# Grouped-query attention: all turns of an odd unit ahead of its second scores

## The chip, the core and the metric

The kernel runs on one core of a Trainium2 chip. The metric is the device time of one execution in microseconds (us). Five instruction streams work side by side and meet at semaphores: TensorE (PE in the rows; PEld is its weight loads), VectorE (DVE), ScalarE (ACT), GpSimd (POOL) and SyncE (SP), which issues most DMAs. TensorE writes its results to PSUM, eight banks of 128 x 512 float32 values here, from where VectorE or ScalarE has to read them before the bank can be written anew.

## The reference, cut to what matters

A two-layer diffusion trunk: layer 0 has neighbourhood attention, layer 1 grouped-query attention (GQA), each followed by a gated ConvFFN. The change touches only the GQA of the 512 latent tokens in layer 1, 16 query heads of width 64 over 4 key heads, with 512 latent and 128 context keys in one softmax:

```
q, k, v = gqa_qkv(h, w_qkv, q_norm, k_norm)      # 512 tokens
q, k = axial_rope(q), axial_rope(k)
k_all = concat([k, cache_k]); v_all = concat([v, cache_v])   # 640 keys
s = einsum('bqkgd,bskd->bkgqs', q, k_all) * hd ** -0.5
p = softmax(s, axis=-1)
o = einsum('bkgqs,bskd->bqkgd', p, v_all)
```

## The kernel before, in words

The latent GQA is cut into 32 units (`NU = 2 * H`). A unit is one head and 256 of the 512 queries. Units alternate between two heads: an even unit u and the odd unit u + 1 are the two heads of a pair with the same queries, and are called a pair below. Each unit has these steps:

- `scores(i)`, i = 0 and 1 (128 queries each): four matmuls of 128 x 320 into the two banks of tile `s2` (in the rows `s`). i = 0 always takes the banks of tag `d0`, i = 1 those of `d1`, and there is one buffer of each. VectorE then finds the row minimum (L1691, of negated scores), ScalarE takes the exponential with its row sum (L1692), VectorE the reciprocal of the sum (L1694) and GpSimd scales (L1695) into `gp`. The next scores of the same i have to wait until the exponential has read the banks.
- `turns(j)`, j = 0, 1, 2 (key chunks 0 and 1, 2 and 3, and 4): four, four and two transposes of 128 x 128 (L120, matmuls against `ident`) into one bank `tp`, which is copied to `pk`. j = 0 is copied by ScalarE (L1706), j = 1 by VectorE (L1708), j = 2 by ScalarE for an even unit and by VectorE for an odd one.
- `values`, once for a pair: the probabilities times the values, accumulated in one bank `po` (20 rows of the trace). Two pairs, the two halves of the queries, share one `po` bank: it is taken at the first pair and given back at the second.

The loop runs over u. At step u it issues the scores of unit u + 2, the turns of unit u, and at an even u the values of units u - 2 and u - 1. `GORDER` (L70) is the order within an even and an odd step: `s0`, `s1` are the scores of unit u + 2, `t0` to `t2` the turns of unit u, `l1` and `l2` the turns 1 and 2 of unit u - 1, left over from the even step, `v` the values, and `p` a piece of the work of the prompt (`sp`, `tq`, `pp`, `ptp`, `opr` in the rows). TensorE keeps the program's order to the letter. The other engines' streams are ordered by a scheduler when the program is built.

The banks: four of the eight hold `s2` (`d0` and `d1`, two each). The other four (pool `psx`) go round in a queue: `Banks.get` takes the bank that was given back longest ago, and each turn gives its bank back as soon as it has issued its copy. With the `po` bank taken there are three for the turns, without it four.

```
        def turns(self, j):
            tp = bk.get("tp")
...
            if j == 0 or j == 2 and self.b == 0:
                nc.scalar.copy(x, tp[:, 0:n])
            else:
                nc.vector.tensor_copy(x, tp[:, 0:n])
            bk.put(tp)
```

From u = 30 on the output projection begins (`m1.part0`, tile `y`), behind the first turn of unit 30: its weights `wr` are rounded to `wh` by ScalarE (L178) and their rest `wl` is made by VectorE (L180), both issued at u = 29.

Of the kernel before, what the change touches and what calls it, by code (L numbers as in the profile page):

```python
# [66 lines left out]
DLEAD = 3  # L67
DPRE = (8, 10, 12, 14)
KP = (2, 2, 2, 2, 1)
GORDER = ("s0 p v s1 t0".split(), "s0 l1 l2 t0 s1 t1 t2".split())  # L70


def raw_ap(ap, offset, dims):
# [31 lines left out]
def hybrid_step(ctx: ExitStack, tc: tile.TileContext, A, O):  # L105
# [1707 lines left out]
    with ExitStack() as s:  # L1813
# [24 lines left out]
        for u in range(NU + 2):  # L1838
            if u + 2 < NU:
                un[u + 2] = Unit(u + 2)  # L1840
            for step in GORDER[u % 2]:
                if step == "p":
# [119 lines left out]
```

## Time and profile before

| what | value |
|---|---|
| time, median of 3 runs | 1548.16 us (1547.85 to 1550.32) |
| the profiled execution: time, span of its instructions | 1550.43 us, 1548.6 us |
| TensorE matmuls busy over the span | 1513.5 us (98%) |
| weight loads, VectorE, ScalarE, GpSimd busy | 1343.4, 1022.3, 854.0, 702.2 us |
| mean granted TensorE clock | 0.998 of full speed |

Busy time is a sum over the whole span. A matmul's end is modelled and matmuls overlap, so where the stream runs without a gap, the distance from one start to the next says what a matmul costs, and its own duration does not.

### The profile page before, as it was taken

The page shows a single profiled execution, that of the slowest core. Times are in us where ns is not written, and L with a number is a line of the kernel's source. Part 1 is how long each engine was busy: PE and PEld are TensorE (multiplying, and loading weights), DVE is VectorE, ACT ScalarE, POOL GpSimd, SP SyncE. Part 2 cuts the span into 40 slices and gives each one's busy share as a digit, 9 for nine tenths or more (in the row PEclk, how much of TensorE's full clock was granted, in tenths as well). Part 3 has the DMA queues.
Part 4 walks back from the last instruction along what each step waited for, and adds up shares of the span by engine and source line. Part 5 has one row for each costly group of instructions (what it writes and reads, how often), then busy time and mean ns, then how long its engine had stood idle before and what let it go on. Part 6 is the DMA issues. An engine that isn't in the chain of part 4 may idle for free.

```text
span 1548.6 us, 26098 instructions
## 1 busy us (share of the span) xinstructions
PE 1513.5 (98%) x9709; PEld 1343.4 (87%) x9709; DVE 1022.3 (66%) x1648; ACT 854.0 (55%) x1624; POOL 702.2 (45%) x606
## 2 busy tenths in 40 slices
PE   6999999999999999999999999999999999999998
PEld 5988998888999999978887878778899999988886
DVE  4553343659877666755757877773988887786554
ACT  5664564646655555554544447763665665564443
POOL 1554564432355455525443464532235666542433
PEclk9999999999999999999999999999999999999999
DMA  9745454253565665388574421015433335447664
GB/s 324 199 123 161 121 134 116 64 189 125 176 225 182 222 190 162 111 279 272 174 238 153 131 67 44 2 34 196 153 115 114 120 110 158 132 161 251 226 220 131
DMA packets 196666, 243.99 MB, mean 158 GB/s; under 512 B 11484, under 2 KB 153020, under 8 KB 196540
## 3 DMA queue, kind: packets, MB, share of 16 engines
q1 hardware_dynamic: 186704, 235.74, 47.8%
q10 hardware_dynamic: 9836, 6.59, 2.5%
q8 instruction: 76, 1.25, 0.3%
q14 instruction: 50, 0.41, 0.1%
HBM read 214.38 MB, written 26.34 MB: 155 GB/s over the span
## 4 chain that ended last, share of the span: by engine, by line
PE 63%; DVE 5%; ACT 2%; issue 2%; POOL 2%; DMA 1%; POOLq 0%; DVEq 0%; ACTq 0%
PE ux L117 18%; PE acc L117 17%; PE uz L117 8%; PE gp L117 5%; PE uy L117 4%; PE po L117 3%; PE y L117 2%; PE s L117 2%; PE tp L120 2%; PE ada L117 1%; DMA wr<-in_ffn_w_down 1%; DVE t L1281 1%; POOL wl L180 1%; DMA wr<-in_ffn_w_up 1%; DVE wl L180 1%
## 5 line engine op out<-in xcount | busy, mean ns | idle before, releaser
L180 POOL TENSOR_TENSOR wl<-wr,wh 128x1024 fp32r<-128x1024 f32 x70 | 173.8, 2487 | 239.8 <-ACT wh L178 228.7
L1204 POOL TENSOR_TENSOR wl<-wr,wh 128x1024 fp32r<-128x1024 f32 x76 | 183.6, 2438 | 46.9 <-ACT wh L1203 43.3
L117 PE MATMUL ux<-B,wh 128*128 128x322 f32 x832 | 200.0, 311 | 0.9 <-ACT u L1258 0.9
L1281 DVE SCALAR_TENSOR_TENSOR t<-C,cw,t 128x644 f32<-128x644 f32 x176 | 156.4, 888 | 51.3 <-ACT t L1279 50.7
L178 ACT CAST wh<-wr 128x1024 fp32r<-128x1024 f32 x140 | 145.5, 1048 | 53.8 <-DMA wr<-in_ffn_w_down 41.1
L117 PE MATMUL acc<-wh,alo 128*128 128x512 f32 x440 | 172.3, 392 | 0.3 <-DVE alo L1173 0.3
L117 PE MATMUL acc<-wl,ahi 128*128 128x512 f32 x440 | 171.9, 391 | 0.5 <-POOL wl L180 0.5
L117 PE MATMUL acc<-wh,ahi 128*128 128x512 f32 x440 | 171.9, 391 | 0.0
L117 PE MATMUL uz<-B,wh 128*128 128x322 f32 x640 | 156.2, 312 | 0.9 <-ACT v L1258 0.9
L117 PEld LDWEIGHTS ux<-B,wh 128*128 128x128 f32 x832 | 143.6, 189 | 3.3 <-issue 1.2
L1173 DVE TENSOR_TENSOR alo<-ain,ahi 128x384 fp32r<-128x384 f32 (+1 forms) x88 | 81.8, 948 | 88.9 <-ACT ahi L1171 88.6
L117 PE MATMUL ux<-B,wl 128*128 128x322 f32 x416 | 129.5, 311 | 3.0 <-DVE wl L1204 3.0
L117 PE MATMUL qk<-hT,wh 128*128 128x384 f32 (+1 forms) x512 | 122.3, 315 | 0.0
L117 PEld LDWEIGHTS uz<-B,wh 128*128 128x128 f32 x640 | 110.9, 189 | 4.4 <-ACT v L1258 1.5
L1204 POOL TENSOR_TENSOR vl<-wr,vh 128x1024 fp32r<-128x1024 f32 x38 | 96.4, 2537 | 24.6 <-ACT vh L1203 24.3
L1203 ACT CAST wh<-wr 128x1024 fp32r<-128x1024 f32 x84 | 84.8, 1049 | 40.9 <-DVE wr L1227 40.6
L1279 ACT ACTIVATE t<-C,cw 128x644 f32<-128x644 f32 x88 | 78.6, 893 | 47.8 <-DVE C L1309 40.2
L180 DVE TENSOR_TENSOR wl<-wr,wh 128x1024 fp32r<-128x1024 f32 x70 | 91.4, 1315 | 19.3 <-ACT wh L178 18.7
L117 PE MATMUL uz<-B,wl 128*128 128x322 f32 x320 | 99.6, 311 | 0.3 <-POOL wl L1204 0.3
L117 PEld LDWEIGHTS acc<-wl,ahi 128*128 128x128 f32 x440 | 82.6, 188 | 18.9 <-POOL wl L180 0.9
L117 PEld LDWEIGHTS acc<-wh,alo 128*128 128x128 f32 x440 | 82.5, 188 | 18.7 <-DVE alo L1173 1.1
L117 PEld LDWEIGHTS acc<-wh,ahi 128*128 128x128 f32 x440 | 82.6, 188 | 17.7
(259 smaller groups left out, 3858.2 us busy)
## 6 DMA issues: line engine op xcount, KB each, us to landing
wr<-in_ffn_w_up SPq DMA_DIRECT2D x88, 512.0 KB
wr<-in_ffn_w_down SPq DMA_DIRECT2D x88, 512.0 KB
wr<-in_ada_w SPq DMA_DIRECT2D x72, 512.0 KB
act<-act SPq DMA_DIRECT2D x44, 321.0 KB
wr<-in_na_w_qkv SPq DMA_DIRECT2D x24, 512.0 KB
mod<-modrow SPq DMA_DIRECT2D x20, 512.0 KB
ain<-act SPq DMA_DIRECT2D x44, 192.0 KB
wf<-in_ada_w SPq DMA_DIRECT2D x16, 512.0 KB
```

Source lines behind the costliest of these rows:

```text
L117: pe(nc.tensor.matmul(*a, **k))
L120: pe(nc.tensor.transpose(*a, **k))
L178: i = nc.scalar.copy(hi, raw)
L180: j = (low or nc.vector).tensor_sub(lo, raw, f32(hi))
L1173: pin(nc.vector.tensor_sub(lo[:, 0 : c1 - c0], ain[:, 0 : c1 - c0], f32(hi[:, 0 : c1 - c0])))
L1203: nc.scalar.copy(hl[0], src)
L1204: low.tensor_sub(hl[1], src, f32(hl[0]))
L1279: nc.scalar.activation(t, taps(0), AF.Identity, bias=cw[:, 3, n : n + 1], scale=cw[:, 1, n : n + 1])
L1281: nc.vector.scalar_tensor_tensor(t, taps(d), cw[:, w, n : n + 1], t, op0=ALU.mult, op1=ALU.add)
```

## The change

In an odd step the second scores of unit u + 2 (`s1`) move from between the turns `t0` and `t1` of unit u to the end of the step. No instruction is added or taken out.

```
-GORDER = ("s0 p v s1 t0".split(), "s0 l1 l2 t0 s1 t1 t2".split())
+GORDER = ("s0 p v s1 t0".split(), "s0 l1 l2 t0 t1 t2 s1".split())
```

The first place is TensorE's stream in an odd step with three banks for the turns (u = 11, at 964 us in the trace of before). `s_10864` are the first scores of unit 13, `s_10892` before and `s_10904` after its second ones, and `s_10917` the first scores of unit 14, which begin the next step; `tp` are the turns.

```order
 L117 MATMUL s_10864<-gkh,gq_9264 128x320 x2
 L117 MATMUL s_10864<-gkl,gq_9264 128x320 x2
-L120 MATMUL tp<-ident,gp 128x128 x10
-L117 MATMUL s_10892<-gkh,gq_9264 128x320 x2
-L117 MATMUL s_10892<-gkl,gq_9264 128x320 x2
-L120 MATMUL tp<-ident,gp 128x128 x6
+L120 MATMUL tp<-ident,gp 128x128 x16
+L117 MATMUL s_10904<-gkh,gq_9264 128x320 x2
+L117 MATMUL s_10904<-gkl,gq_9264 128x320 x2
 L117 MATMUL s_10917<-gkh,gq_9263 128x320 x2
 L117 MATMUL s_10917<-gkl,gq_9263 128x320 x2
```

The sixteen turns (five banks taken one after another, `l1`, `l2`, `t0`, `t1`, `t2`) now follow each other without scores in between, and the two scores stand back to back.

The second place is VectorE's stream in the same step. The first `COPY` of 128x512 is that of `l1`, the other two are those of `t1` and `t2`.

```order
 L1694 RECIPROCAL rcg<-sug 128x1
 L1708 COPY pk<-tp 128x512
-L1691 TENSOR_REDUCE nmg<-s_10892 128x1
-L1694 RECIPROCAL rcg<-sug 128x1
-L1708 COPY pk<-tp 128x512
-L1708 COPY pk<-tp 128x256
-L1694 RECIPROCAL rcg<-sug 128x1
+L1694 RECIPROCAL rcg<-sug 128x1
+L1708 COPY pk<-tp 128x512
+L1708 COPY pk<-tp 128x256
+L1691 TENSOR_REDUCE nmg<-s_10904 128x1
 L1691 TENSOR_REDUCE nmg<-s_10917 128x1
```

What stands ahead of the copy of `l1` is the same; the reduction of the second scores moves behind the copies of `t1` and `t2`.

The third place is ScalarE's stream at the end of the units (u = 29): `s_11760` are the first and `s_11788` (before) or `s_11800` (after) the second scores of the last unit, 31, and `wh` are the weights of the output projection.

```order
 L1692 ACTIVATE gp,sug<-s_11740,nmg 128x640
 L1706 COPY pk<-tp 128x256
-L1706 COPY pk<-tp 128x512
 L1692 ACTIVATE gp,sug<-s_11760,nmg 128x640
-L1692 ACTIVATE gp,sug<-s_11788,nmg 128x640
+L1706 COPY pk<-tp 128x512
+L1692 ACTIVATE gp,sug<-s_11800,nmg 128x640
 L178 CAST wh<-wr 128x1024 x4
 L1706 COPY pk<-tp 128x512
```

The weights are still rounded behind the exponential of the last scores, whichever place these have in TensorE's stream.

## Rows read from the trace of the kernel before

**Rows 1.** Busy us of PE, PEld, DVE, ACT, POOL; granted clock; the stretch of the units:

```profile
923.00:1036.00 113.00, 110.07 (x855) 89.92 (x854) 84.66 (x179) 81.23 (x194) 53.80 (x70) 1.00 0.06 20
```

**Rows 2.** Waits from 923 to 1036 us: total, times, longest (us):

```profile
PEld s L117 <- ACT gp L1692: 6.9, 13, 1.2
...
PEld tp L120 <- DVE pk L1708: 1.3, 6, 0.2
```

**Rows 3.** Timeline of u = 11, three banks: start, duration, then what ran:

```profile
965.45 0.56 PE L117 MATMUL s<-gkh,gq 128*128 128x320 f32 x2
965.51 0.69 DVE L1708 COPY pk<-tp 128x512 f32<-128x512 f32 x1
...
966.25 0.87 PE L120 MATMUL tp<-ident,gp 128*128 128x128 f32 x6
...
966.88 0.53 PE L117 MATMUL s<-gkh,gq 128*128 128x320 f32 x2
...
967.55 0.60 PE L120 MATMUL tp<-ident,pp 128*128 128x128 f32 x4
```

**Rows 4.** Timeline of u = 7, three banks, no wait for a bank:

```profile
948.80 0.68 DVE L1708 COPY pk<-tp 128x512 f32<-128x512 f32 x1
...
950.83 0.38 PE L120 MATMUL tq<-ident,qt 128*128 128x128 f32 x2
```

**Rows 5.** Timeline of u = 9, four banks (the last row begins the prompt's scores):

```profile
956.89 0.68 DVE L1708 COPY pk<-tp 128x512 f32<-128x512 f32 x1
...
957.51 0.56 PE L117 MATMUL s<-gkh,gq 128*128 128x320 f32 x2 [0.87 <-ACT gp L1692]
...
959.44 0.22 PE L117 MATMUL sp<-gkh,gq 128*128 128x128 f32 x1
```

**Rows 6.** Timeline of u = 1, the first of eight odd steps with four banks:

```profile
926.44 0.67 DVE L1708 COPY pk<-tp 128x512 f32<-128x512 f32 x1
...
927.69 0.54 PE L117 MATMUL s<-gkh,gq 128*128 128x320 f32 x2
```

**Rows 7.** Timeline, scores right behind scores, then the matmul after them:

```profile
911.95 0.46 PE L117 MATMUL s<-gkh,gq 128*128 128x320 f32 x2
...
912.54 0.40 PE L117 MATMUL gp<-wh,hT 128*128 128x512 f32 x1
```

**Rows 8.** Timeline of u = 29, the last odd step with scores, and what follows:

```profile
1034.58 0.54 PE L117 MATMUL s<-gkh,gq 128*128 128x320 f32 x2
...
1034.77 0.67 DVE L1708 COPY pk<-tp 128x512 f32<-128x512 f32 x1
...
1036.00 2.64 PE L117 MATMUL po<-pk,gvt 128*64 128x256 f32 x20
...
1036.31 0.79 ACT L1692 ACTIVATE gp<-s,nmg 128x640 f32<-128x640 f32 x1
...
1037.10 3.88 ACT L178 CAST wh<-wr 128x1024 fp32r<-128x1024 f32 x4
...
1038.16 2.42 DVE L180 TENSOR_TENSOR wl<-wr,wh 128x1024 fp32r<-128x1024 f32 x2 [0.68 <-ACT wh L178]
...
1039.50 0.50 PE L117 MATMUL y<-wl,ph 128*128 128x512 f32 x1
```

**Rows 9.** Timeline, transposes in a row, two groups at the start:

```profile
17.00 1.06 PE L120 MATMUL tr<-ident,x 128*128 128x128 f32 x8 [1.54 <-DVE x L541]
18.47 1.69 PE L120 MATMUL tr<-ident,x 128*128 128x128 f32 x8 [0.41 <-DVE x L541]
```

**Rows 10.** Columns of rows 1: the second group of rows 9; u = 31's turns:

```profile
18.47:20.10 1.63, 1.63 (x10) 1.30 (x10) 0.45 (x1) 0.59 (x1) 0.00 (x0) 0.58 1.09 365
...
1048.90:1050.60 1.70, 1.70 (x18) 1.70 (x16) 0.69 (x1) 0.72 (x2) 0.00 (x0) 1.00 1.01 405
```

**Rows 11.** TensorE's longest waits from 1036 us to the end:

```profile
PE ux L117 <- DVE wl L1204: 1.3, 1, 1.3
PE ux L117 <- DVE C L1307: 1.2, 1, 1.2
```

## The prediction

> **What bounds the kernel now.** I first read busy time and clock over the stretch of the units: TensorE is busy 110.07 of 113 us at full clock [rows 1], so time is lost or won here only through its gaps, or through the order of its own work. The waits of this stretch come next [rows 2]: the weight loads of scores waited 6.9 us for the exponential that has to read their banks, and six turns waited 1.3 us together for a copy by VectorE. The first is what the change moves away from: second scores that arrive before the exponential has read `d1`. The second decides, in my reading, what comes in its place. So I then read the timeline of single odd steps, TensorE's and VectorE's rows side by side.
>
> Why do turns wait for VectorE? The `tp` banks are given out in the order in which they came back. A pair takes six: one for `t0` of the even step, then `l1`, `l2`, `t0`, `t1`, `t2` of the odd one. With three banks (`po` held) `t0` gets the bank of the even step's `t0`, and `t1` that of `l1`. With four, `t1` gets the bank of the even step's `t0`, and `t2` that of `l1`. So one of the last two turns always needs the bank of `l1`, which VectorE copies only behind the reductions of two scores. By the loop, u = 3, 7, ... 27 are seven steps with three banks, and u = 1, 5, ... 29 are eight with four.
>
> **The change part by part.** No instruction comes or goes, SP's work is the same, and so is GpSimd's but for its place; the cost lies in what TensorE waits for and in the order of its work. Call L the end of the copy of `l1`. On VectorE nothing ahead of this copy moves (the second order piece), so I take L as it is.
>
> *Three banks.* At u = 11 the copy of `l1` starts at 965.51 and ends at 966.20; the second scores start at 965.45 without a wait, and `t1` at 966.25, 0.05 after L; `t1` and `t2` take 0.63 up to 966.88, the next first scores 0.67 up to 967.55 [rows 3]. So before, the step ends at L + 0.05 + 0.63 + 0.67 = L + 1.35, and the second scores stood in time in which `t1` could not have run anyway. After, `t1` stands where they stood and waits for L all the same, about 0.8 us (965.45 to 966.25). The second scores come behind `t2` for 0.67, and the next first scores, now right behind scores, take 0.59 (911.95 to 912.54 [rows 7]): L + 0.05 + 0.63 + 0.67 + 0.59 = L + 1.94. That is 0.59 us more, and for all six steps with a wait in the second row of [rows 2] it is the same sum. The seventh had no such wait, but there the copy ends at 948.80 + 0.68 = 949.48, so the new end is 951.42 against 950.83 [rows 4], again 0.59. Seven times 0.59 is 4.13 us.
>
> *Four banks.* Here `t2` waits for L, and behind it come two turns (a third of 0.63, 0.21), and the scores: L + 0.05 + 0.21 + 0.67 + 0.59 = L + 1.52. At u = 9, where the second scores waited longest, 0.87 us, L is 957.57, the new end 959.09 and the old 959.44: a gain of 0.35 [rows 5]. At u = 1 L is 927.11, the new end 928.63, the old one 927.69 + 0.67 = 928.36: a loss of 0.27 [rows 6]. At u = 29 no first scores follow: L = 1035.44, the values start at L + 0.05 + 0.21 + 0.67 = 1036.37 instead of 1036.00, a loss of 0.37 [rows 8]. The other five, read in the same way, gain 0.05 to 0.09 each, 0.3 together. The eight come to nothing: the wait for the exponential is gone, and the wait for the bank is as long.
>
> *The end of the units.* The exponential of the last second scores stands ahead of the four roundings `wh` on ScalarE (third order piece), and the output projection's second product waits for the first `wl`. From the start of these scores to that product it is 4.92 us (1034.58, exponential 1036.31, `wh` 1037.10, `wl` 1038.16, product 1039.50 [rows 8]). Before, the values started 1.42 us behind these scores' start, with six turns in between, and the product 3.50 behind the values' start. Now only the scores' own 0.67 lie ahead of the values, and the product comes 4.92 - 0.67 = 4.25 behind their start: +0.75 us. If ScalarE could hide it, this term would be nothing.
>
> *What I cost at nothing.* The later exponential of the second scores: `d1` is needed again by the next step's second scores, 0.67 + 0.59 us and the values (up to 2.64 with their modelled end) behind, 3.9 us in all. Reduction and exponential end 1.73 + 0.79 = 2.5 us after the scores' start [rows 8], and the copy of `t1` (0.69) may now stand in front: 3.2 us. Some 0.7 us of cover are left. Pieces of the prompt's work on ScalarE could eat it; if each of 15 steps lost a tenth, it would be 1.5 us more, which I keep for the upper end. GpSimd's scaling of an odd unit has a whole pair's time until its turns.
>
> **Sum:** 4.13 + 0.0 + 0.75 = +4.9 us. The profiled execution took 1550.43 us, so it would take 1555.3; it is 2.3 us above the median of the three runs, and against the median it is 1548.16 + 4.9 = **1553.1 us** (+0.32%). A measurement of this kernel can tell about 0.2%, 3.1 us, from no change.
>
> **The rivals.** *The delay is lost again later.* After the units TensorE waits only in a few places, 1.3 and 1.2 us at the longest [rows 11]. If their releasers did not move along, these would take up 2.5 us, and +2.4 is left: 1550.6 us, no change that can be told. The same verdict follows if L comes earlier by 0.3 us in the seven steps (7 x 0.3 = 2.1, so 1551.0). Against it: `wl` at L1204 and `C` at L1307 hang on weights and on results of TensorE's own earlier products, which come later too, and the copy of `l1` follows its reductions at once.
>
> *The banks are free in time.* If VectorE copied `l1` before `t1` or `t2` needs it, the move would only take waits away. At the best all 6.9 + 1.3 us of waits vanish and the end costs 0.75: 1540.7 us. I count half of the 8.2, since first scores are among those that waited: 1548.16 - 4.1 + 0.75 = 1544.8, faster. It decides in the three-bank steps: the copy would have to end 0.8 us sooner than at 966.20, before the second scores' old place at 965.45 [rows 3]. It takes 0.69 itself and stands behind two reductions, so the rows leave little for it.
>
> *The clock falls.* Sixteen transposes in a row are new in 15 steps. In the first stage eight transposes took 1.69 us where the granted clock was 0.58 in the mean, part of it at the lower level of 1.2 GHz, and 1.06 us at 17.00 [rows 9, 10]. If every run of sixteen, now 1.7 us, were stretched in this ratio, 1.6, each would lose 1.0 us and the 15 steps 15 us: 1568 us with the loss above. The trace has such a run behind 1048.90, and its granted clock is 1.00, the upper level of 2.4 GHz [rows 10]; so this gets a small chance. The Trainium skill ("TensorE: Matmul & The Clock Gate", Part 4: PE-mode transpose) says that transposes do not count as busy in the way other matmuls do, and that the full clock does not engage for them. By that page the time would be nearer to 1568 us; the trace does not agree, with 1.00 through the run at 1048.90.
>
> That the change does nothing is excluded by the order of the built program.
>
> **How the numbers follow.** I give the forecast 0.70, the lost delay (or a copy that comes sooner) 0.22, the banks free in time 0.06, the clock 0.02. The forecast's own range is 1551.0 (without the 0.75 of the end and 1.4 less for the spread of the runs shown) to 1556.0 (with the 1.5 and as much spread). Its lowest edge, 0.02, still counts as no change. So faster is 0.06, the same 0.22 + 0.02 = 0.24, slower 0.68 + 0.02 = 0.70. The range goes down over the lost delay to 1548.3 and up to 1555.8; outside lie the gain, the clock and the outer edges of the others, together under 0.2.
>
> **What would show it.** In the waits of the same stretch the 6.9 us of scores for the exponential should shrink to about 2 us, and the turns' wait for the copy at L1708 should grow from 1.3 us in six places to 7 to 11 us in some fifteen. From one start of the values to the next, a pair with three banks should take 0.6 us more than before, and one with four about as much as before, but for u = 9, which should be shorter by 0.35. The first product with `wl` should follow the values' start by 4.2 us. The forecast is wrong if the turns wait for ScalarE or not at all, or if the values start later because copies of `t1` and `t2` are late.

## The result, and the profile after

The changed kernel took 1554.24 us (median of 9 runs, 1553.01 to 1556.89) against 1548.16 (9 runs, 1546.32 to 1550.49): a ratio of 1.0039, interval 1.0031 to 1.0048. It is slower, by 4.8 to 7.4 us. The profiled execution took 1553.34 us, its span is 1551.2 us. Measured once more later, it came to 1554.88 us, ratio 1.0041 (1.0028 to 1.0054).

TensorE's work did not grow; this is the busy row of the page after:

```profile
PE 1511.9 (97%) x9709; PEld 1342.4 (87%) x9709; DVE 1026.2 (66%) x1648; ACT 851.4 (55%) x1624; POOL 699.0 (45%) x606
```

The stretch of the units, in the columns of [rows 1], again from 0.2 us ahead of the first turn of unit 0 to the start of the last values:

```profile
920.42:1037.05 116.63, 110.06 (x855) 89.64 (x854) 85.40 (x181) 79.32 (x195) 53.36 (x70) 1.00 0.06 19
```

Busy time is the same to 0.01 us, the granted clock is 1.00 as before, and the stretch is 3.63 us longer. All of it is time in which TensorE stood still: 116.63 - 110.06 = 6.57 us, against 113.00 - 110.07 = 2.93. The waits after, of weight loads (PEld) and of the matmuls themselves (PE), from 920 to 1037 us:

```profile
PEld tp L120 <- DVE pk L1708: 9.2, 15, 0.9
PEld s L117 <- ACT gp L1692: 5.5, 12, 1.2
PE tp L120 <- DVE pk L1708: 5.3, 12, 0.7
...
PE s L117 <- ACT gp L1692: 1.2, 2, 0.9
```

The turns' wait for VectorE's copy of `l1` went from 1.3 us in six places [rows 2] to 9.2 in fifteen, one for each odd step. The matmuls themselves stood 5.3 us for it. In return, the matmuls' wait for the exponential fell to 1.2 us in two places: 0.24 on the scores just ahead of the stretch, which this view still takes in, and 0.93 on the first scores of step u = 1, where the kernel before has 0.94 too. The 5.3 and the 0.93 make 6.2 of the 6.57 us. In a second profile of the kernel before, the same row, with the same two places in it, reads:

```profile
PE s L117 <- ACT gp L1692: 3.2, 8, 0.9
```

So 2.0 us of waiting for the exponential went and 5.3 for the bank came. The step u = 11, with three banks, answers to [rows 3]:

```profile
963.96 0.67 DVE L1708 COPY pk<-tp 128x512 f32<-128x512 f32 x1
...
964.69 0.87 PE L120 MATMUL tp<-ident,gp 128*128 128x128 f32 x6 [0.57 <-DVE pk L1708]
...
965.32 0.54 PE L117 MATMUL s<-gkh,gq 128*128 128x320 f32 x2
...
965.98 0.46 PE L117 MATMUL s<-gkh,gq 128*128 128x320 f32 x2
...
966.57 0.60 PE L120 MATMUL tp<-ident,pp 128*128 128x128 f32 x4
```

The copy of `l1` ends at 964.63 (L). `t1` starts 0.06 behind it, after a wait that now has nothing in it; the second and the next first scores follow, and the step is through at 966.57 = L + 1.94. The step u = 9, with four banks, answers to [rows 5]:

```profile
954.08 1.69 PE L120 MATMUL tp<-ident,gp 128*128 128x128 f32 x14
...
955.72 0.68 DVE L1708 COPY pk<-tp 128x512 f32<-128x512 f32 x1
...
956.46 0.44 PE L120 MATMUL tp<-ident,gp 128*128 128x128 f32 x2 [0.69 <-DVE pk L1708]
956.65 0.54 PE L117 MATMUL s<-gkh,gq 128*128 128x320 f32 x2
...
957.90 0.22 PE L117 MATMUL sp<-gkh,gq 128*128 128x128 f32 x1
```

Fourteen transposes run through, and the last two, those of `t2`, wait for the copy that ends at 956.40. The end is at L + 1.50; before it was at 959.44 with L at 957.57, L + 1.87. The end of the units, which answers to [rows 8]:

```profile
1036.29 0.53 PE L117 MATMUL s<-gkh,gq 128*128 128x320 f32 x2
...
1036.98 0.67 DVE L1708 COPY pk<-tp 128x512 f32<-128x512 f32 x1
1037.05 2.54 PE L117 MATMUL po<-pk,gvt 128*64 128x256 f32 x20
1037.57 0.81 DVE L1691 TENSOR_REDUCE nmg<-s 128x1 f32<-128x640 f32 x1
1038.42 0.80 ACT L1692 ACTIVATE gp<-s,nmg 128x640 f32<-128x640 f32 x1 [1.26 <-DVE nmg L1691]
...
1041.55 0.50 PE L117 MATMUL y<-wl,ph 128*128 128x512 f32 x1 [0.76 <-DVE wl L180]
```

The values start 0.76 behind the last second scores, and the first product with `wl` 4.50 behind the values, against 3.50.

From the first turn of unit 0 to that product it is 120.93 us after (920.62 to 1041.55) and 116.30 before (923.20 to 1039.50), and second profiles of both kernels give 120.94 and 116.29. This stretch repeats to 0.01 us, so parts of a microsecond can be read in it that the total time cannot tell. It is taken apart at the starts of the values; around u = 11 these are, in the kernel before and then in the changed one:

```profile
960.38 2.38 PE L117 MATMUL po<-pk,gvt 128*64 128x256 f32 x20
...
968.08 2.38 PE L117 MATMUL po<-pk,gvt 128*64 128x256 f32 x20
```

```profile
958.83 2.38 PE L117 MATMUL po<-pk,gvt 128*64 128x256 f32 x20
...
967.09 0.65 PE L117 MATMUL po<-pk,gvt 128*64 128x256 f32 x4
```

This pair lasted 7.70 us before and lasts 8.26 now, 0.56 more. All of the 4.63 us, term by term:

| term | predicted, us | measured, us |
|---|---|---|
| seven pairs with three banks | +4.13 | +4.15 (0.56 to 0.71 each) |
| u = 1 and seven pairs with four banks | 0.0 | -0.52 |
| last values to the first product with `wl` | +0.75 | +1.00 |
| sum | +4.9 | +4.63 |

### The profile page after: what moved, and what is told of

The parts are those of the page before. It is cut to its first block, busy times and chain, and to the rows that moved or that the text cites. A ratio compares the mean times of both kernels' runs of the same rounds, so it can differ in the third digit from the quotient of the medians.

```text
span 1551.2 us, 26078 instructions
## 1 busy us (share of the span) xinstructions
PE 1511.9 (97%) x9709; PEld 1342.4 (87%) x9709; DVE 1026.2 (66%) x1648; ACT 851.4 (55%) x1624; POOL 699.0 (45%) x606
## 4 chain that ended last, share of the span: by engine, by line
PE 77%; DVE 8%; DMA 4%; ACT 3%; issue 3%; POOL 3%; SPq 0%; POOLq 0%; ACTq 0%; DVEq 0%
PE ux L117 18%; PE acc L117 15%; PE uz L117 8%; PE y L117 6%; PE gp L117 5%; PE uy L117 5%; PE qk L117 4%; PE po L117 4%; PE vp L117 3%; PE s L117 3%; PE tp L120 2%; PE ada L117 2%; DVE nmg L1691 1%; POOL wl L180 1%; DMA wf<-in_ada_w 1%
## 5 line engine op out<-in xcount | busy, mean ns | idle before, releaser
L1204 POOL TENSOR_TENSOR wl<-wr,wh 128x1024 fp32r<-128x1024 f32 x76 | 183.5, 2437 | 48.4 <-ACT wh L1203 44.7
L1204 POOL TENSOR_TENSOR vl<-wr,vh 128x1024 fp32r<-128x1024 f32 x38 | 96.0, 2525 | 24.6 <-ACT vh L1203 24.3
```

Of the source, the lines that this page charges most:

```text
L1204: low.tensor_sub(hl[1], src, f32(hl[0]))
```

## The experiments

Theory A, the bank: one of the last two turns of an odd step needs the bank of `l1`, whose copy stands behind two reductions on VectorE; the second scores used to stand in that wait, and now it is bare. Theory B, the late scores: the second scores come later, so do their reduction and exponential, and these pile up and hold back the scores of the next steps, about 0.3 us in each of 15 odd steps. All ten kernels compute everything; they differ in the order of an odd step alone. In the diffs `GORDER` has one entry for each u % 4 (1: odd steps with four banks, 3: with three) and, where there is a fifth, one for u = 29; the even entries are as before.

| kernel | median, us | ratio to before | stretch against 116.3, us |
|---|---|---|---|
| before again | 1548.77 | 0.9998 (0.9989 to 1.0007) | 0.0 |
| change again | 1554.88 | 1.0041 (1.0028 to 1.0054) | +4.6 |
| three banks only | 1553.33 | 1.0028 (1.0017 to 1.0039) | +3.9 |
| four banks only | 1551.27 | 1.0018 (1.0010 to 1.0027) | +0.8 |
| half way, three banks | 1553.20 | 1.0027 (1.0018 to 1.0036) | +3.3 |
| change, `l2` first | 1552.79 | 1.0028 (1.0018 to 1.0038) | +2.9 |
| before, `l2` first | 1548.42 | 1.0000 (0.9991 to 1.0009) | -0.7 |
| change but u = 29 | 1553.88 | 1.0034 (1.0022 to 1.0046) | +3.6 |
| mix | 1548.64 | 0.9999 (0.9991 to 1.0008) | -0.9 |
| mix with `l2` first | 1547.73 | 0.9994 (0.9985 to 1.0003) | -2.0 |

**The change in the steps with three banks alone.**

```diff
+ 1: s0 l1 l2 t0 s1 t1 t2   (as before)
+ 3: s0 l1 l2 t0 t1 t2 s1
```

> The order of the change in the seven odd steps with three banks for the turns (u = 3, 7, ... 27), the order of before in the other eight. Theory A (one of the last turns waits for the bank of l1, and with three banks the moved scores used to fill that wait): +0.59 us in each of the seven steps, +4.1 us, nothing in the others and nothing at the end; 1552.3 us, ratio 1.0027; turns wait for the copy at L1708 in seven places with 0.5 to 0.9 us each. Theory B (it is the late second scores themselves: their reduction and exponential come later and pile up with those of the next first scores, whatever the banks): the cost is shared over the fifteen steps by count, 7/15 of the 5.2 us that the stretch and its end lost, +2.4 us, ratio 1.0016.

Each of the seven pairs lost 0.57 to 0.60 us, 4.07 together, and all other terms came to -0.2. The waits of the turns for the copy in this kernel's stretch:

```profile
PEld tp L120 <- DVE pk L1708: 5.5, 7, 0.8
```

Seven waits for seven steps. A's size to a few hundredths, and twice what B allows.

**The change in the steps with four banks alone.**

```diff
+ 1: s0 l1 l2 t0 t1 t2 s1
+ 3: s0 l1 l2 t0 s1 t1 t2   (as before)
```

> The order of the change in the eight odd steps with four banks (u = 1, 5, ... 29), the order of before in the seven with three. Theory A: the steps gain 0.5 us together, the end of the units costs 1.0 us; +0.5 us, ratio 1.0003, no difference that can be told. Theory B: 8/15 of the loss, +2.8 us, ratio 1.0018.

The stretch lost 0.81 us: the eight steps +0.08, the pairs between +0.13, the end +0.60. The sum is near A's 0.5, but its parts are not as A had them. The steps did not gain 0.5: u = 5 and u = 25, which gain about 0.3 each with the whole change, are as before here, and u = 29 loses 0.44. And the end costs 0.60 instead of 1.00, since the reduction of the last second scores starts 0.86 us behind them here (1036.22 to 1037.08), and 1.28 with the whole change. The total time came out with B's number, 1.0018, though. Part of it lies outside the units (below), and the two measures do not agree better than 1 to 2 us; since the loss that B speaks of would have to be in the stretch, it is not there.

**Half of the move.** This one tells the theories apart most sharply: the second scores pass one turn instead of two.

```diff
+ 1: s0 l1 l2 t0 s1 t1 t2   (as before)
+ 3: s0 l1 l2 t0 t1 s1 t2
+ 29: as before
```

> Only the seven steps with three banks differ from before, and only half as far as in the change: s0 l1 l2 t0 t1 s1 t2, the second scores one turn later instead of two. Bank theory (A): t1 still waits for the bank of l1 with nothing ahead of it; behind the end L of that copy come t1 (0.42), the second scores (0.67), t2 (0.21) and the next first scores (0.67), L + 0.05 + 1.97 = L + 2.02 against L + 1.35 before: 0.67 us a step, 4.7 us in all, more than the whole change costs there (3.85 measured); the pairs with three banks last 7.9 to 8.4 us. Late-scores theory (B): the second scores are late by less than half as much, so at most half of the 3.85: 1.9 us. Away from the units, both allow 0.6 us for the later wait of the last ConvFFN that all changed orders but one showed. Ratio to before: A 1.0030 to 1.0035, B 1.0012 to 1.0016.

The seven pairs lost 0.56 to 0.60 each, 4.02 together: half the move costs as much as the whole. For B this is twice too much. The timeline of u = 11 in this kernel:

```profile
963.83 0.67 DVE L1708 COPY pk<-tp 128x512 f32<-128x512 f32 x1
...
964.56 0.66 PE L120 MATMUL tp<-ident,gp 128*128 128x128 f32 x4 [0.57 <-DVE pk L1708]
...
964.97 0.54 PE L117 MATMUL s<-gkh,gq 128*128 128x320 f32 x2
...
965.64 0.38 PE L120 MATMUL tp<-ident,gp 128*128 128x128 f32 x2
965.78 0.54 PE L117 MATMUL s<-gkh,gq 128*128 128x320 f32 x2
...
966.44 0.60 PE L120 MATMUL tp<-ident,pp 128*128 128x128 f32 x4
```

The same bare wait of 0.57 stands ahead of `t1`, and the step ends at L + 1.94 (964.50 to 966.44), as with the whole change. A's L + 2.02 was a little high: `t2` between two scores takes 0.14 here, not 0.21.

**The bank taken away.** With `l1` and `l2` exchanged, the turn that waited gets the bank of `l2`, half the size and copied by ScalarE.

```diff
- odd: s0 l1 l2 t0 t1 t2 s1   (the change)
+ odd: s0 l2 l1 t0 t1 t2 s1
```

> The change with l2 ahead of l1 in the odd step (s0 l2 l1 t0 t1 t2 s1): the second scores stay last and behind nothing new, but with three banks t1 now gets the bank of l2, which ScalarE copies, and only t2 that of l1; with four banks t2 gets that of l2. Theory A: with three banks a step ends 0.42 us earlier than with the change alone (two turns are left behind the wait instead of six), 2.9 us in seven, and with four banks the wait for VectorE goes, 0.1 to 0.6 us in most steps; 3 to 5 us faster than the change, so 1549 to 1551 us, ratio 1.001 to 1.002; turns wait for L1708 in seven places instead of fifteen, under 4 us instead of 9.2. Theory B: the scores are as late as with the change, 1554 us, ratio 1.004.

No turn waits for VectorE's copy any more (A had left seven such waits), and the seven pairs with three banks cost 1.36 us against 4.15: the wait was the bank, as A has it. The waits that came in its place, from 920 to 1041 us:

```profile
PE s L117 <- ACT gp L1692: 3.7, 8, 0.9
...
PEld tp L120 <- ACT pk L1706: 2.3, 7, 0.6
...
PE tp L120 <- ACT pk L1706: 0.4, 1, 0.4
```

The seven turns now wait for ScalarE's copy of `l2`, but the matmuls stand still for it at u = 7 alone, whose pair makes 0.55 of the 1.36. A's forecast of 3 to 5 us was still missed: the stretch only won 1.71 us of 4.63, since the steps with four banks now took 1.1 more than with the change, which A had not foreseen. Such a step in this kernel:

```profile
971.55 1.91 PE L120 MATMUL tp<-ident,gp 128*128 128x128 f32 x16
...
973.18 0.59 ACT L1706 COPY pk<-tp 128x512 f32<-128x512 f32 x1
973.22 0.55 PE L117 MATMUL s<-gkh,gq 128*128 128x320 f32 x2
...
973.66 0.80 ACT L1692 ACTIVATE gp<-s,nmg 128x640 f32<-128x640 f32 x1
...
974.60 0.56 PE L117 MATMUL s<-gkh,gq 128*128 128x320 f32 x2 [0.55 <-ACT gp L1692]
```

Sixteen transposes run through and the second scores follow at once. Now the next step's first scores come so early that `d0` is not free: ScalarE made the copy of `t0` (973.18) ahead of the exponential that reads it (973.66). One wait is gone, the next one stands 1.4 us behind it.

```diff
- odd: s0 l1 l2 t0 s1 t1 t2   (before)
+ odd: s0 l2 l1 t0 s1 t1 t2
```

> The order of before with l1 and l2 exchanged alone: s0 l2 l1 t0 s1 t1 t2. The waiting turns now need the bank of l2, half the size and copied by ScalarE. A: the six short waits of turns for VectorE's copy (1.3 us) vanish, nothing else changes; 0.1 to 1.0 us shorter than before, ratio 0.9993 to 1.000. In the changed order the same exchange took 1.7 us from the stretch, which by A is a saving only because the bank wait stood bare there. B: the exchange itself is worth 1.7 us in either order, ratio 0.9989.

In the order of before the same exchange is worth 0.71 us: 0.15 to 0.18 in six of the seven pairs with three banks, none in the seventh, and 0.3 lost with four banks. The six waits of 1.3 us are gone. B's 1.7 is not seen; the exchange is worth much where the wait is bare, and little where scores stand in it.

**The last odd step.** The change, but u = 29 with the order of before.

```diff
  1, 3: s0 l1 l2 t0 t1 t2 s1   (the change)
+ 29: s0 l1 l2 t0 s1 t1 t2
```

> The change, but for u = 29, the last odd step with scores, which keeps the order of before. Theory A with the term of the end: 0.25 us for the step and 1.0 us for the later rounding of the projection's weights come back, 1.2 us less than with the change, 1553.0 us, ratio 1.0031; the first product with wl follows the values' start by 3.5 us, not 4.5. Theory B says nothing of the end; if the end costs nothing (ScalarE's work is hidden by the next products), the time is that of the change, 1554.2 us.

From the values' start to the product with `wl` this kernel takes 3.45 us again:

```profile
1039.20 2.50 PE L117 MATMUL po<-pk,gvt 128*64 128x256 f32 x20
...
1042.65 0.50 PE L117 MATMUL y<-wl,ph 128*128 128x512 f32 x1
```

So in the changed order the place of the second scores in this one step makes the 1.0 us of the end. The step itself gave nothing back (its pair lasts 6.90 us, 6.83 with the change, 6.58 before): its second scores start 0.31 us later behind the values than in the kernel before, 0.18 of it in a wait for the exponential of the changed step ahead.

**Against both kernels.** If A is right, the second scores may be moved back as long as they still stand ahead of the turn that waits: with four banks that is `t2`.

```diff
+ 1: s0 l1 l2 t0 t1 s1 t2
+ 3, 29: s0 l1 l2 t0 s1 t1 t2   (as before)
```

> Steps with three banks and the last odd step as before; steps with four banks take the order s0 l1 l2 t0 t1 s1 t2, in which the only turn that waits for the bank of l1 still has the second scores ahead of it, but these come four transposes (0.42 us) later than before and so nearer to the time at which their exponential has freed the banks. Bank theory (A): the waits for the exponential shrink and no new wait for the bank comes: the stretch is 0.9 to 1.7 us shorter than the 116.3 of before, ratio 0.9990 to 0.9994. Late-scores theory (B): any step later for the second scores costs; seven steps by about a third of the 0.3 us that it gives to each of 15 steps: 0.7 us longer, ratio 1.0005.

The stretch is 0.9 us shorter, the lower edge of what A said, and the pairs with u = 9 to 21 gain 0.19 to 0.45 each. In the total nothing of it is seen: 0.9999 (0.9991 to 1.0008), where A had 0.9990 to 0.9994. With the exchange in the steps with three banks as well:

```diff
+ 1: s0 l1 l2 t0 t1 s1 t2
+ 3: s0 l2 l1 t0 s1 t1 t2
+ 29: as before
```

> What gained in two runs put together: steps with four banks s0 l1 l2 t0 t1 s1 t2 (0.9 us less in the stretch), steps with three banks s0 l2 l1 t0 s1 t1 t2 (0.13 to 0.18 less in each pair, seven of them: 1.1), the last odd step as before. A: the stretch is 1.5 to 2.2 us shorter than 116.3 us; total 1546.4 to 1547.0 if nothing later takes it up, 1547.0 to 1547.6 if the last ConvFFN's wait grows by 0.6 us; ratio 0.9987 to 0.9994. B: the second scores of the four-bank steps are later, no gain there; 0 to 1 us, ratio 0.9994 to 1.0000.

It is 1.96 us shorter, the shortest of all, and in the total 0.9994 (0.9985 to 1.0003): the best order found, by a gain that the timing does not separate from no change.

**The same kernels once more.** The unchanged kernel against itself shows what the timing can tell.

> The kernel before once more, unchanged, against itself. Both theories (bank of l1; late second scores) expect a ratio of 1.000 within 0.001. What it is for: the four variants so far lost 0.5 to 2.0 us more against the kernel before than their units' stretch (first turn of unit 0 to the first product with wl) explains, and before's one profile began this stretch at 923.2 us where three of the four variants began it at 920.6 to 922.7. If that difference is only the one profile of before, its second profile has the same 116.3 us (within 0.3) in the stretch and a start that differs from 923.2 by 0.5 us or more; if the changed orders also make something ahead of the stretch differ, its start is 923.2 again.

> The changed kernel once more, unchanged. Both theories: 1.0039 within 0.001 of the kernel before; 120.9 us (within 0.3) from the first turn of unit 0 to the first product with wl. Its place for what lies outside this stretch: if outside nothing differs, its total less the total of the unchanged kernel's second profile is 4.6 us within 0.5; if the change costs outside too, it is 6 us.

The kernel before gave 0.9998, and 116.29 us in the stretch, with the first turn at 921.32 instead of 923.20. The changed kernel began it at 920.62 and at 922.04. So the part ahead of the units differs by 1.4 to 1.9 us between two executions of one program, and a difference of that size there cannot be put down to the change. The profiled totals of the two kernels lie 1554.74 - 1547.49 = 7.3 us apart here (neither the 4.6 nor the 6 of the expectation) and 1553.34 - 1550.43 = 2.9 us in the first pair: one pair of profiles cannot give the sum, the stretch can.

## Why the prediction was right, point by point

- **Three banks, 0.59 each.** Right in mechanism and size: 4.15 for 4.13, and L + 1.94 at u = 11 to the hundredth. The largest loss, 0.71, is that of u = 7, where L itself came 0.12 us later behind the values than before (5.76 for 5.64). The changes in the steps with three banks alone (4.07), half way (4.02) and with `l2` first (1.36) show that it is the bank of `l1` and not the lateness of the second scores.
- **Four banks, nothing.** The mechanism held (wait for the bank in place of the wait for the exponential), the size was off by 0.5. u = 1 lost 0.26 (0.27 predicted), u = 29 0.25 (0.37), u = 9 gained 0.24 (0.35). The five others were put at 0.05 to 0.09 each; three gained 0.07, but u = 5 and u = 25 0.30 and 0.28. With the change in the steps with three banks alone these two gained 0.22 and 0.20 already, with the change in their own kind alone 0.01 at most: their wait for the exponential was partly inherited from the step with three banks ahead of them, which I had read as their own. It shows in L, which I took as it was: counted from the start of the values ahead, it came 0.20 us earlier at u = 5, 25 and 29 (5.82 for 6.02) and 0.14 later at u = 9 (6.35 for 6.21). With the change in the steps with three banks alone L moved in the same way (5.82 and 6.36), with the change in the steps with four alone it stayed (6.02 and 6.20). In ten of the 15 steps it moved by 0.02 or less.
- **End of the units, 0.75.** The step was right and mis-sized: 1.00. I took 4.92 us from the last second scores to the product from [rows 8]; it was 5.26. On VectorE their reduction now also stands behind the copies of `t2` and `t1` (1036.98) and starts 1.28 behind the scores; the exponential starts 2.13 behind them, before 1.73. The order of VectorE's stream has this; I had read ScalarE's alone there.
- **The later exponential, nothing.** Right: behind the first scores of step u = 1 no matmul of the stretch waits for an exponential.
- **The sum.** 4.63 for 4.9 is closer than its terms are, and partly luck: the two that were mis-sized, by -0.52 and by +0.25, lie on opposite sides.
- **What I said the waits would show.** The turns' 9.2 us in 15 places was in the forecast. The loads of scores were to fall to about 2 us and fell to 5.0 in the stretch itself (the 5.5 above have one wait ahead of it); ten of the 11 waits left are of 0.38 to 0.39, behind the values, where the matmuls themselves lose nothing. I should have taken the row of the matmuls (3.2 to 1.2).
- **The rivals.** The banks were not free in time: fifteen waits. The granted clock stayed at 1.00, the level of 2.4 GHz, over the stretch, and the fourteen transposes in a row at u = 9 took 1.69 us, 0.12 each; the sixteen at 971.55 with `l2` first took 1.91, 0.12 each too. The rule of the Trainium skill that was set against the trace ("TensorE: Matmul & The Clock Gate", Part 4: PE-mode transpose) would have made these runs slower; the trace does not agree. The delay was not won back behind the units. The waits there, for [rows 11]:

```profile
PE ux L117 <- DVE C L1307: 1.2, 1, 1.2
...
PE ux L117 <- DVE wl L1204: 1.1, 1, 1.1
...
PE uz L117 <- ACT v L1258: 0.7, 1, 0.7
```

The first two are those of [rows 11], at nearly the same length. The third grew from 0.19 us in the first profile of the kernel before: 0.56 us more were lost there (last section). With it the traces explain 4.63 + 0.56 = 5.2 us of the 6.1 between the medians, inside the interval of 4.8 to 7.4. The forecast was 1.1 us under the median. In the other kernels that differ from before the median also lies 0.1 to 1.1 us above what the traces explain, for the steps with four banks alone just outside its interval; where that comes from stays open.

## What to carry to other kernels

A wait that moved work would take away may be the cover of another one: before moving a block out from ahead of an instruction, ask when that instruction could have run anyway (here when the buffer came free that is handed out in turn), and price the move as the difference of the two. When a rotation of buffers is shared by consumers of different speed, the turn that gets the slow one's buffer decides, and which turn that is changes with the number of buffers. Measure such a change in its own stretch, between two events that the change does not touch: there it repeated to 0.01 us, while whole executions of one program differ by 2 to 6 us.

## What the runs showed of the hardware that I had not expected

Some 330 us behind the units, in the last ConvFFN, the engines' programs are in the same order before and after, and yet TensorE lost 0.56 us. VectorE and GpSimd each have a subtraction that reads two tiles in SBUF there (`al` and `vl`, L1204). First in the second profile of the kernel before, then in the changed one:

```profile
1363.44 0.78 DVE L1204 TENSOR_TENSOR al<-wr,ah 128x512 fp32r<-128x512 f32 x1
1363.61 2.88 POOL L1204 TENSOR_TENSOR vl<-wr,vh 128x1024 fp32r<-128x1024 f32 x1
...
1364.93 2.11 DVE L1224 TENSOR_TENSOR wr<-wr 128x512 f32<-128x512 f32 x1
```

```profile
1367.14 2.44 POOL L1204 TENSOR_TENSOR vl<-wr,vh 128x1024 fp32r<-128x1024 f32 x1
1367.23 2.90 DVE L1204 TENSOR_TENSOR al<-wr,ah 128x512 fp32r<-128x512 f32 x1
...
1370.84 0.68 DVE L1224 TENSOR_TENSOR wr<-wr 128x512 f32<-128x512 f32 x1
```

Before, VectorE was 0.17 us ahead, was through in 0.78, and a later sum (L1224) was held for 2.11 us. After, GpSimd was 0.09 ahead, and VectorE's subtraction took 2.90 us, until 0.55 behind the end of GpSimd's. The Trainium skill ("SBUF — State Buffer", SBUF: two separate sides) says that a VectorE instruction with two inputs in SBUF and a GpSimd instruction that reads SBUF share a pair of ports as a lock, which the one that starts first keeps for its whole instruction. The trace agrees: VectorE's subtraction took 0.78 us where it was first and 2.90 where it was second, GpSimd's 2.44 where it was first and 2.88 where it was second. Where the two starts lie 0.02 us apart or less, the record's order does not tell which is held: VectorE's, first by 0.02, took 2.99 us in the change with three banks alone (at 1354.50), and first by 0.01 only 0.69 in the mix (at 1350.25). So VectorE's sum (L1224) ended 329.97 us behind the first product with `wl` in the changed kernel, and 329.43 in the second profile of the kernel before; and in the changed one the product with `uz` had to wait for ScalarE's copy of `v`:

```profile
1386.56 0.42 ACT L1258 COPY v<-uz 128x322 f32<-128x322 f32 x1
1387.03 0.41 PE L117 MATMUL uz<-B,wh 128*128 128x322 f32 x1 [0.75 <-ACT v L1258]
```

In the first profile of the kernel before it waited 0.19 there:

```profile
1384.62 0.42 PE L117 MATMUL uz<-B,wh 128*128 128x322 f32 x1 [0.19 <-ACT v L1258]
```

Nine of the twelve profiles have the longer wait, both mixes among them; the two of the kernel before and that of before with `l2` first have not. In eight of the nine GpSimd's subtraction started first; in the ninth, the change in the steps with three banks alone, VectorE's was 0.74 us ahead, but fell into the GpSimd subtraction before (`wl`), which ran on for 0.82 us: it took 1.37, again until 0.55 behind GpSimd's end, and the sum was held for 2.11 all the same. In the nine the sum ended 329.97 to 330.21 us behind the first product with `wl`, in the three 329.43 to 329.61. So where VectorE's subtraction falls against GpSimd's is a cause read from the traces, not shown: no kernel was made that sets it by itself, and why the phase of the engines shifts with the order of the units is open.
